# Forgetting attention: copying and scaling both halves of a unit's output at once, the second half added in DRAM by an accumulating transfer

## Chip, cores and metric

The kernel runs on one core of a Trainium2 chip. The metric is the device time of one execution in microseconds (us), as a median over runs. The engines are TensorE (PE, with its weight loads PEld), VectorE (DVE), ScalarE (ACT), GpSimd (POOL) and SyncE (SP), which issues most DMAs.

## What is computed

One layer of an encoder trunk on a sequence of 2048 tokens of width 1024: a mixing block of two halves (eight heads of "forgetting" attention and a multi-scale pool), attention over 256 memory tokens, and a gated feed-forward block. The change concerns the eight heads only:

```python
def forgetting_attention(q, k, v, f_logit):      # q, k, v: (B, H, S, Dh), here H = 8, S = 2048, Dh = 64
    c = cumsum(log_sigmoid(f_logit))
    for start in range(0, S, Q_BLOCK):           # causal: keys up to the query
        s = einsum('bhqd,bhkd->bhqk', qb, kb) * scale
        s = s + c[:, :, start:end, None] - c[:, :, None, :end]
        p = softmax(where(kpos <= qpos, s, -inf))
        outs.append(einsum('bhqk,bhkd->bhqd', p, vb))
```

## The kernel before

All products are computed in float32 accuracy from pairs of words: a number is split into a rounded high part and a low part that holds the rest, and a product is a sum of matmuls of the parts.

The attention stage, some 380 us of the program, works through 32 units, one for each head h (0 to 7) and each block b (0 to 3) of 512 queries. A unit has two sides. On the score side (score_items), for each 128 queries and each 512 keys, PE makes a tile of scores (L791), VectorE adds the forgetting term and tracks the row's extreme (L793, over several chunks reduced by L798), and ACT takes the exponential with row sums (L803). POOL cuts the causal mask into the forgetting term (cm, L782). On the value side (value_items), for each 128 keys, PE turns the weights (tp, L56), ACT casts the high part ph from PSUM (L891), VectorE subtracts the low part pl (L64), and PE multiplies both with the values into an accumulator acc (L854). Of every eighth chunk ACT copies the weights (pf, L887) and POOL makes both parts (L888, and L64 on POOL). The last chunk of a unit covers only 128 of its 256 columns, so POOL zeroes the others of ph and pl beforehand (L880).

A head's values are stored with 128 columns: 64 for the high part of the values and 64 for the low part. So rows 0 to 63 and rows 64 to 127 of acc are two addends of one result, and something has to add them. When a unit's last chunk is multiplied, finish copies rows 64 to 127 to SBUF on ACT (fo, L830) and adds rows 0 to 63 on VectorE (L831). Later scale multiplies fo by 1/l, the inverse of the row sums, on POOL (L837), and POOL's own queue writes it to the DRAM tensor catT (L839), one tensor for each b, 64 rows for each head. After attention the output projection reads catT (load_cat, L736).

The inverse takes a way of its own: POOL adds two partial sums (li, L817), VectorE takes the reciprocal (L818), SP stores the column to DRAM (ld, L819) and reads it back as a row broadcast to all partitions (lbs, L825).

What sets the order: PE, DVE and ACT run in the order in which the code issues (in_order). A loop takes a score item and a value item in turn, the scores 22 items ahead, and each item is a tick. Work can be put off by a number of ticks with later(n, fn): a scale comes 12 ticks after finish, the broadcast load 22 after the reciprocal. POOL and SP aren't in that list: a scheduler places their instructions by priority and readiness when the program is built. Each engine then executes its own list strictly in order, and an instruction that waits for a semaphore holds everything behind it on that engine.

Also on SP: the loads of the next head's queries, keys and forgetting row (L588 to L592, issued with unit (h, 1)) and of the next head's values (L582, unit (h, 3)).

Of the kernel before, what the change touches and what calls it, by code (L numbers as in the profile page):

```python
# [8 lines left out]
F32 = mybir.dt.float32  # L9
F32R = mybir.dt.float32r  # L10
AF = mybir.ActivationFunctionType
ALU = mybir.AluOpType
# [4 lines left out]
P = 128  # L17
# [4 lines left out]
H = 8  # L22
DH = 64
# [18 lines left out]
def block_kernel(ctx: ExitStack, tc: tile.TileContext, x, xT, memT, cols, rows, w_qkvf, w_p, w_pool, w_out,  # L42
# [4 lines left out]
    act, dve, pool, pe, sp = nc.scalar, nc.vector, nc.gpsimd, nc.tensor, nc.sync  # L47

    def opened(stack, name, bufs=1, **kw):
        return stack.enter_context(tc.tile_pool(name=name, bufs=bufs, reuse_waits="tile", **kw))  # L50
# [61 lines left out]
    ld = [dr.tile([P, 4], F32, name=f"ld{n}") for n in range(4 * H)]  # L112
    mkvd = dr.tile([4, P, 1024], F32, name="mkvd")
    catT = [dr.tile([FOXW, 512], F32, name=f"catT{n}") for n in range(4)]
# [605 lines left out]

    EX, X2, INV = 7, 2, 2

    BACK, SCALE = 22, 12

    SHARE = 8

    rest, last_parts = [], []
    hpb = opened(hps, "hpb")
# [14 lines left out]
    with ExitStack() as c0:  # L743
        spool = opened(c0, "spool")
        tpool = opened(c0, "tpool")
# [5 lines left out]
        def later(n, fn):  # L751
            due.append([n, fn])
# [16 lines left out]
        def score_items(unit):  # L769
# [6 lines left out]
            for q in range(4):  # L776
# [8 lines left out]
                for c in range(b + 1):  # L785
# [9 lines left out]
                    if c == b:  # L795
# [11 lines left out]
                        if n > 1024:  # L807
                            later(EX + X2, lambda expo=expo: expo(g=1))
                    yield True
            later(EX + X2 + INV, lambda: inverse(unit))  # L810

        def inverse(unit):

            h, b = unit["u"]
            l = unit["l"]
            li = tpool.tile([P, 4], F32, tag="li", name="li", bufs=8)
            pool.tensor_tensor(out=li[:], in0=l[:, :, 0], in1=l[:, :, 1], op=ALU.add)  # L817
            dve.reciprocal(li[:], li[:])  # L818
            sp.dma_start(ld[4 * h + b], li[:])  # L819
            later(BACK, lambda: inverse_back(unit))  # L820

        def inverse_back(unit):
            h, b = unit["u"]
            unit["lb"] = lbs = tpool.tile([DH, 512], F32, tag="lbs", name="lbs", bufs=3)
            sp.dma_start(lbs[:], ld[4 * h + b].rearrange("t q -> (t q)").partition_broadcast(DH))  # L825

        def finish(unit, acc):
            h, b = unit["u"]
            fo = tpool.tile([DH, 512], F32, tag="fo", name="fo", bufs=3)
            act.copy(fo[:], acc[DH:, :])  # L830
            dve.tensor_tensor(out=fo[:], in0=acc[:DH, :], in1=fo[:], op=ALU.add)  # L831
            later(SCALE, lambda: scale(unit, fo))

        def scale(unit, fo):
            h, b = unit["u"]

            pool.tensor_tensor(out=fo[:].rearrange("p (q t) -> p q t", q=4), in0=fo[:].rearrange("p (q t) -> p q t", q=4),  # L837
                               in1=unit["lb"][:].rearrange("p (t q) -> p q t", q=4), op=ALU.mult)
            pool.dma_start(catT[b][h * DH:(h + 1) * DH, :], fo[:])  # L839

        nchunk = [0]

        def value_items(unit):
# [20 lines left out]
            for j in range(nk):  # L864
# [18 lines left out]
                lag = LAG  # L883
                if nchunk[0] % SHARE == 0 and 0 < j < nk - 4 and not (h == H - 1 and b >= 2):
                    lag += 2
# [11 lines left out]
            def drain():  # L897
                step(True)
                finish(unit, acc)
# [728 lines left out]
```

## Time and profile before

| what | value |
|---|---|
| median of 3 runs | 2525.05 us (2523.53 to 2525.37) |
| the profiled execution | 2526.31 us |
| its span, first to last instruction | 2524.6 us |
| PE, DVE, ACT, POOL busy over the span | 99%, 67%, 49%, 32% |
| granted clock of PE | 1.00 |
| attention, first score matmul to last value matmul | 520.9 to 901.0 us |

The profile is one execution seen by the hardware profiler. Its timeline rows give start, duration, engine, line, operation and what is written from what, then in brackets the engine's idle time before the row and who ended it. Its table of waits has the total, the number of times and the longest. Its table of groups has the number of instructions, busy time and mean in ns, then idle time before them. PE's matmuls are pipelined: a 512-column matmul is shown as 0.39 us or more, though the next may start 0.23 us after it, so PE's pace is read from the distances of starts, not from durations. POOL's spans are rough.

### The profile page before, as it was taken

How to read it: one execution, taken by the hardware profiler on the slowest of the kernel's cores; microseconds unless marked ns; L12 is line 12 of the kernel's file. 1: busy time of each engine (PE TensorE's matmuls, PEld its weight loads, DVE VectorE, ACT ScalarE, POOL GpSimd, SP SyncE). 2: the span in 40 equal slices, each digit the busy share in tenths (PEclk: the TensorE clock that was granted, in tenths of full speed). 3: DMA queues.
4: the chain of work that ended last, by engine and by line, in shares of the span. 5: the costliest groups of instructions: out<-in, count | busy, mean ns of one | idle time of the engine just before them, and what ended most of it. 6: DMA issues, size and time to landing. Idle time of an engine off the chain costs nothing.

```text
span 2524.6 us, 36797 instructions
## 1 busy us (share of the span) xinstructions
PE 2501.6 (99%) x13055; PEld 2139.0 (85%) x13055; DVE 1690.1 (67%) x2999; ACT 1241.4 (49%) x2355; POOL 796.4 (32%) x1096
## 2 busy tenths in 40 slices
PE   9999999999999999999999999999999999999999
PEld 8999999878888878888888888888888888888887
DVE  7444485579999965445877887756776666665554
ACT  6454451069999945444544433335543333333443
POOL 3344310035554623334244554430011212212000
PEclk9999999999999999999999999999999999999999
DMA  6454474364464241223654544457673323325665
GB/s 248 155 156 129 126 240 163 130 180 136 114 170 126 72 134 69 87 88 105 226 203 155 200 163 179 167 190 267 231 254 109 113 96 125 113 96 186 234 205 204
DMA packets 204504, 400.38 MB, mean 159 GB/s; under 512 B 24480, under 2 KB 100000, under 8 KB 193440
## 3 DMA queue, kind: packets, MB, share of 16 engines
q1 hardware_dynamic: 175104, 301.54, 37.0%
q0 software_dynamic: 29216, 96.49, 9.9%
q8 instruction: 102, 1.67, 0.3%
q14 instruction: 82, 0.67, 0.1%
HBM read 273.05 MB, written 129.11 MB: 159 GB/s over the span
## 4 chain that ended last, share of the span: by engine, by line
PE 70%; issue 9%; DVE 3%; ACT 2%; POOL 1%; DMA 0%; SPq 0%; POOLq 0%; DVEq 0%; ACTq 0%
PE bk L71 14%; PE bk L69 14%; PE bk L70 14%; PE acc L854 5%; PE sps L791 4%; PE tp L56 3%; PE mmps L69 3%; PE mmps L71 3%; PE mmps L70 3%; PE oo L69 1%; PE oo L70 1%; PE oo L71 1%; PE zp L69 1%; PE zp L70 1%; PE zp L71 1%
## 5 line engine op out<-in xcount | busy, mean ns | idle before, releaser
L64 DVE TENSOR_TENSOR ww<-draw,ww 128x512 fp32r<-128x512 f32 x308 | 204.6, 702 | 157.2 <-ACT ww L190 156.9
L190 ACT CAST ww<-draw 128x512 fp32r<-128x512 f32 x308 | 179.1, 620 | 220.4 <-PE bk L71 177.7
L64 DVE TENSOR_TENSOR ww<-graw,ww 128x512 fp32r<-128x512 f32 x220 | 177.6, 814 | 107.5 <-ACT ww L190 107.3
L69 PE MATMUL bk<-ww,ww 128*128 128x512 f32 x616 | 239.6, 389 | 0.0
L70 PE MATMUL bk<-ww,ww 128*128 128x512 f32 x616 | 239.6, 389 | 0.0
L71 PE MATMUL bk<-ww,ww 128*128 128x512 f32 x616 | 239.6, 389 | 0.0
L190 ACT CAST ww<-graw 128x512 fp32r<-128x512 f32 x220 | 136.0, 622 | 177.2 <-PE bk L71 159.8
L64 DVE TENSOR_TENSOR pl<-tp,ph 128x512 fp32r<-128x512 f32 (+3 forms) x298 | 177.2, 598 | 16.6 <-ACT ph L891 15.3
L69 PE MATMUL zps<-wh,xhi 128*128 128x384 f32 (+1 forms) x512 | 174.4, 341 | 0.6 <-DVE qs L186 0.6
L70 PE MATMUL zps<-wl,xhi 128*128 128x384 f32 (+1 forms) x512 | 171.9, 336 | 0.0
L71 PE MATMUL zps<-wh,xl 128*128 128x384 f32 (+1 forms) x512 | 171.9, 336 | 0.0
L891 ACT CAST ph<-tp 128x512 fp32r<-128x512 f32 (+3 forms) x298 | 147.9, 517 | 12.2 <-PE tp L56 9.0
L69 PE MATMUL bk<-qs,ww 128*128 128x512 f32 x352 | 137.9, 392 | 0.8 <-ACT s L1440 0.8
L1521 POOL DMA_DIRECT2D out_dram<-o x32 | 17.3, 542 | 382.7 <-DVE o L1518 377.0
L71 PE MATMUL bk<-qs,ww 128*128 128x512 f32 x352 | 137.2, 390 | 0.8 <-DVE ww L64 0.8
L70 PE MATMUL bk<-kh,ww 128*128 128x512 f32 x352 | 137.0, 389 | 0.0
L69 PE MATMUL bk<-kl,ww 128*128 128x512 f32 x352 | 136.9, 389 | 0.0
L70 PE MATMUL bk<-cb,ww 128*128 128x512 f32 x352 | 136.9, 389 | 0.0
L71 PE MATMUL bk<-kl,ww 128*128 128x512 f32 x352 | 136.9, 389 | 0.0
L69 PEld LDWEIGHTS bk<-ww,ww 128*128 128x128 f32 x616 | 115.6, 188 | 24.2
L71 PEld LDWEIGHTS bk<-ww,ww 128*128 128x128 f32 x616 | 115.6, 188 | 24.1
L70 PEld LDWEIGHTS bk<-ww,ww 128*128 128x128 f32 x616 | 115.6, 188 | 23.8
(635 smaller groups left out, 7238.5 us busy)
## 6 DMA issues: line engine op xcount, KB each, us to landing
graw<-in_w_gu_dram SPq DMA_DIRECT2D x44, 1024.0 KB, 5.4
draw<-in_w_down_dram SPq DMA_DIRECT2D x66, 256.0 KB, 4.3
xl<-in_xT_dram SPq DMA_DIRECT2D x64, 256.0 KB, 5.1
qkT<-st SPq DMA_DIRECT2D x64, 256.0 KB, 2.7
wdr<-in_w_down_dram SPq DMA_DIRECT2D x22, 512.0 KB, 4.4
vd<-cb SPq DMA_DIRECT2D x16, 512.0 KB, 3.3
qs<-qkT SPq DMA_DIRECT2D x8, 1024.0 KB, 7.0
kh<-qkT SPq DMA_DIRECT2D x16, 512.0 KB, 9.7
```

Of the source, the lines that this page charges most:

```text
L56: return pe.transpose(out.bitcast(F32R), src, identr[:])
L64: (eng or dve).tensor_tensor(out=lo, in0=src, in1=f(hi), op=ALU.subtract)
L69: pe.matmul(ps, lhsT=sh, rhs=mh, start=first, stop=False, skip_group_check=goes_on)
L70: pe.matmul(ps, lhsT=sh, rhs=ml, start=False, stop=False, skip_group_check=goes_on)
L71: pe.matmul(ps, lhsT=sl, rhs=mh, start=False, stop=last, skip_group_check=goes_on)
L190: act.copy(hi, raw)
L791: pe.matmul(ps[:, :wn], lhsT=qs[:, i * P:(i + 1) * P], rhs=kk[:, 512 * c:512 * c + wn], start=(a == 0), stop=(a == 1))
L854: pe.matmul(acc[:, qa * P:], lhsT=v[:, j, :], rhs=pm[:, qa * P:], start=state["n"] == 1, stop=state["n"] == 2 * nk)
L891: act.copy(ph[:, sl], tp[:, sl])
L1521: pool.dma_start(out[rows_, cs], o)
```

## The change

For the heads 0 to 6 (28 units) ACT copies all 128 rows of acc at once, and VectorE's add is left out. POOL scales all 128 rows, for which the broadcast of 1/l now goes to 128 partitions. SP writes the first 64 rows plainly to catT; 8 ticks after that POOL issues a transfer of the other 64 rows to the same place, which adds to what is there. This transfer must wait until SP's write has landed. Head 7 keeps the old way. The reciprocal and the store of its result come 4 ticks later than before, and the broadcast load 18 ticks after that instead of 22, so at the same tick.

```diff
-    BACK, SCALE = 22, 12
-
-    SHARE = 8
+    BACK, SCALE, ADDED = 22, 12, 8
+
+    SHARE, RECIP = 8, 4
...
-            dve.reciprocal(li[:], li[:])
-            sp.dma_start(ld[4 * h + b], li[:])
-            later(BACK, lambda: inverse_back(unit))
+
+            def turned_over():
+                dve.reciprocal(li[:], li[:])
+                sp.dma_start(ld[4 * h + b], li[:])
+                later(BACK - RECIP, lambda: inverse_back(unit))
+
+            later(RECIP, turned_over)
...
-            unit["lb"] = lbs = tpool.tile([DH, 512], F32, tag="lbs", name="lbs", bufs=3)
-            sp.dma_start(lbs[:], ld[4 * h + b].rearrange("t q -> (t q)").partition_broadcast(DH))
+            unit["lb"] = lbs = tpool.tile([P, 512], F32, tag="lbs", name="lbs", bufs=3)
+            sp.dma_start(lbs[:], ld[4 * h + b].rearrange("t q -> (t q)").partition_broadcast(P))
...
-            fo = tpool.tile([DH, 512], F32, tag="fo", name="fo", bufs=3)
-            act.copy(fo[:], acc[DH:, :])
-            dve.tensor_tensor(out=fo[:], in0=acc[:DH, :], in1=fo[:], op=ALU.add)
+            fo = tpool.tile([P, 512], F32, tag="fo", name="fo", bufs=3)
+            if h < H - 1:
+                act.copy(fo[:], acc[:])
+            else:
+                act.copy(fo[:DH], acc[DH:])
+                dve.tensor_tensor(out=fo[:DH], in0=acc[:DH], in1=fo[:DH], op=ALU.add)
...
-            pool.tensor_tensor(out=fo[:].rearrange("p (q t) -> p q t", q=4), in0=fo[:].rearrange("p (q t) -> p q t", q=4),
-                               in1=unit["lb"][:].rearrange("p (t q) -> p q t", q=4), op=ALU.mult)
-            pool.dma_start(catT[b][h * DH:(h + 1) * DH, :], fo[:])
+            rows = P if h < H - 1 else DH
+
+            pool.tensor_tensor(out=fo[:rows].rearrange("p (q t) -> p q t", q=4), in0=fo[:rows].rearrange("p (q t) -> p q t", q=4),
+                               in1=unit["lb"][:rows].rearrange("p (t q) -> p q t", q=4), op=ALU.mult)
+            cat = catT[b][h * DH:(h + 1) * DH, :]
+            (sp if h < H - 1 else pool).dma_start(cat, fo[:DH])
+            if h < H - 1:
+                later(ADDED, lambda: pool.dma_start(cat, fo[DH:], accum_op=ALU.add))
```

What it moves on the engines, first POOL, where the units (h, 3) and (h + 1, 0) end. catT_118 and catT_115 are the DRAM tensors of block 3 and block 0; li and l belong to the row sums, cm is the mask. Before:

```order
L880 MEMSET ph 128x128
L837 TENSOR_TENSOR fo<-fo,lbs 64x512
L839 DMA catT_118<-fo 64x512
L880 MEMSET pl 128x128
L782 AFFINE_SELECT cm<-cb 128x384
L817 TENSOR_TENSOR li<-l 128x4
L837 TENSOR_TENSOR fo<-fo,lbs 64x512
L773 MEMSET l 128x8
L839 DMA catT_115<-fo 64x512
L888 TENSOR_TENSOR ph<-pf,ones 128x512
L782 AFFINE_SELECT cm<-cb 128x512
L64 TENSOR_TENSOR pl<-pf,ph 128x512
```

And now, where L850 is the accumulating transfer, L845 the scale and L891 the memset (L880 before):

```order
L845 TENSOR_TENSOR fo<-fo,lbs 128x512
L891 MEMSET ph 128x128
L891 MEMSET pl 128x128
L782 AFFINE_SELECT cm<-cb 128x384
L845 TENSOR_TENSOR fo<-fo,lbs 128x512
L850 DMA catT_118<-fo 64x512
L817 TENSOR_TENSOR li<-l 128x4
L773 MEMSET l 128x8
L782 AFFINE_SELECT cm<-cb 128x512
L899 TENSOR_TENSOR ph<-pf,ones 128x512
L64 TENSOR_TENSOR pl<-pf,ph 128x512
L850 DMA catT_115<-fo 64x512
```

The scale stands ahead of both memsets, the DMA issue that stood between them is gone, and the accumulations come behind the next scale and behind the shared chunk; the memsets of unit (h, 1) follow right after the last row shown.

On SP, before (ld_85 to ld_88 hold 1/l of the units (0, 3), (1, 0), (1, 1) and (1, 2), lbs is the broadcast, v the values, catT_117 the tensor of block 2):

```order
L819 DMA ld_85<-li 128x4
L819 DMA ld_86<-li 128x4
L825 DMA lbs<-ld_85 64x512
L825 DMA lbs<-ld_86 64x512
L819 DMA ld_87<-li 128x4
L825 DMA lbs<-ld_87 64x512
L582 DMA v<-vd 128x2048
L819 DMA ld_88<-li 128x4
L825 DMA lbs<-ld_88 64x512
```

And now, with the plain writes of catT (L848) among them:

```order
L821 DMA ld_85<-li 128x4
L821 DMA ld_86<-li 128x4
L848 DMA catT_117<-fo 64x512
L829 DMA lbs<-ld_85 128x512
L829 DMA lbs<-ld_86 128x512
L821 DMA ld_87<-li 128x4
L582 DMA v<-vd 128x2048
L829 DMA lbs<-ld_87 128x512
L848 DMA catT_118<-fo 64x512
L848 DMA catT_115<-fo 64x512
L821 DMA ld_88<-li 128x4
L829 DMA lbs<-ld_88 128x512
```

Each plain write waits for a scale on POOL and stands ahead of broadcasts; the write of block 3 is behind the load of the values.

On VectorE only the add goes and the reciprocals shift by a few rows; the end of unit (0, 0), as a difference:

```order
 L793 ISA s3g_5485,mx<-sps,cb 128x512
 L793 ISA mx 128x1
-L831 TENSOR_TENSOR fo<-acc,fo 64x512
 L64 TENSOR_TENSOR pl<-tp,ph 128x512
 L793 ISA s3g_5485,mx<-sps,cm 128x128
```

The low part (L64) now follows the scores' row directly. ACT's and PE's orders are unchanged.

## The prediction

> **What bounds the kernel now.** First the page: TensorE (PE) is busy all the time, so only time in which PE stands still inside the attention stage can be won or lost.
>
> ```profile
> span 2524.6 us, 36797 instructions
> PE 2501.6 (99%) x13055; PEld 2139.0 (85%) x13055; DVE 1690.1 (67%) x2999; ACT 1241.4 (49%) x2355; POOL 796.4 (32%) x1096
> ```
>
> The span is 2524.6 us of an execution of 2526.3; the median of the runs shown is 2525.05, so I add the sum's difference to that median. 0.2% of it is 5.05 us, about what a measurement of this kernel can tell from no change.
>
> Next the busy times by stretch inside attention (520 to 901 us). Columns: the stretch, its length, then PE, PEld, DVE, ACT and POOL busy.
>
> ```profile
> 660.00:700.00 40.00, 39.83 (x256) 33.31 (x254) 38.30 (x124) 36.32 (x78) 21.26 (x41) 1.00 0.40 127
> ```
>
> Three engines are nearly full: PE 39.8, DVE 38.3 and ACT 36.3 of 40 us; the clock is full (1.00). POOL is half idle. Third, who waited for whom over five heads (586 to 818 us):
>
> ```profile
> PEld tp L56 <- DVE pl L64: 4.3, 15, 0.4
> PEld acc L854 <- POOL pl L880: 1.9, 5, 0.4
> ```
>
> PE's losses are two a head: once on POOL's memset (L880), and on VectorE's low part (L64). The timeline of head 3 gives their size. PE at the last value chunk of the unit (h, 0), and POOL there:
>
> ```profile
> 675.67 1.57 POOL L837 TENSOR_TENSOR fo<-fo,lbs 64x512 f32<-64x512 f32 x1 [1.51 <-DVE fo L831]
> ...
> 677.54 0.57 POOL L839 DMA_DIRECT2D catT<-fo  x1 [0.29 <-POOL fo L837]
> ...
> 677.94 0.28 PE L854 MATMUL acc<-ph,v 128*128 128x256 f32 x1
> ...
> 678.11 0.22 POOL L880 MEMSET pl<- 128x128 f32 x1
> ...
> 678.38 0.39 PE L854 MATMUL acc<-pl,v 128*128 128x256 f32 x1 [0.16 <-POOL pl L880]
> ...
> 678.61 0.46 PE L56 MATMUL tp<-identr,s1g 128*128 128x128 f32 x4
> ```
>
> Matmuls of 256 columns otherwise start 0.12 us apart; this one comes 0.44 after the last and the next 0.23 later: 0.43 us lost, because the scale and the DMA issue stand ahead of the memset. The other loss comes at 704:
>
> ```profile
> 702.31 0.58 ACT L830 COPY fo<-acc 64x512 f32<-64x512 f32 x1
> ...
> 702.92 1.07 ACT L891 CAST ph<-tp 128x512 fp32r<-128x512 f32 x2
> 702.93 0.68 DVE L831 TENSOR_TENSOR fo<-acc,fo 64x512 f32<-64x512 f32 x1
> ...
> 703.54 0.69 DVE L64 TENSOR_TENSOR pl<-tp,ph 128x512 fp32r<-128x512 f32 x1
> ...
> 703.73 0.34 PE L791 MATMUL sps<-kh,qs 128*128 128x384 f32 x1
> ...
> 703.90 0.34 PE L791 MATMUL sps<-kl,qs 128*128 128x384 f32 x1
> ...
> 704.29 0.54 PE L56 MATMUL tp<-identr,s3g 128*128 128x128 f32 x4
> ```
>
> A 384-column matmul needs 0.17 us before its successor (703.73 to 703.90), and the next one gets 0.39: with the late transposes about 0.25 us are lost. The low part at 703.54 ends it, and the final add L831 stands directly ahead of it. But the low part also needs the high part that ACT casts from 702.92, behind its own copy of the output. A cast of 512 columns takes 0.59 (row 679.82 below), so the first of the two in that row ends at 703.51, and the low part starts at 703.54. Without the add it would start 0.03 us earlier. **The add is hidden behind ACT's cast.** What is late here is ACT. Its waits between 674 and 705:
>
> ```profile
> 674.28 0.59 ACT L830 COPY fo<-acc 64x512 f32<-64x512 f32 x1 [0.71 <-PE acc L854]
> ...
> 683.03 1.15 ACT L803 ACTIVATE s3g<-s3g,mx 128x1024 f32<-128x1024 f32 x1 [0.46 <-DVE mx L798]
> ...
> 686.88 1.15 ACT L803 ACTIVATE s3g<-s3g,mx 128x1024 f32<-128x1024 f32 x1 [0.31 <-DVE mx L798]
> ...
> 692.18 1.15 ACT L803 ACTIVATE s3g<-s3g,mx 128x1024 f32<-128x1024 f32 x1 [0.34 <-DVE mx L798]
> ```
>
> These four are all the idle spells that the view marks there. ACT waits for PE at 674.28 and then for nothing but VectorE until PE runs into it at 704.29. One head earlier the same stall stood here:
>
> ```profile
> 657.93 0.54 PE L56 MATMUL tp<-identr,s3g 128*128 128x128 f32 x4
> ```
>
> A head thus takes 704.29 - 657.93 = 46.36 us, and for 30 of them the pace is ACT's, with PE a little ahead; only the 16 from 657.93 to 674.28 are PE's.
>
> **The change part by part.** *VectorE's add* (28 of 32 go):
>
> ```profile
> L837 POOL TENSOR_TENSOR fo<-fo,lbs 64x512 f32<-64x512 f32 x32 | 50.6, 1582 | 39.3 <-DVE fo L831 39.3
> L888 POOL TENSOR_TENSOR ph<-pf,ones 128x512 fp32r<-128x512 f32 x22 | 23.1, 1051 | 0.5 <-ACT pf L887 0.2
> L831 DVE TENSOR_TENSOR fo<-acc,fo 64x512 f32<-64x512 f32 x32 | 21.8, 680 | 1.0 <-ACT fo L830 1.0
> ```
>
> 28 x 0.68 = 19.0 us of VectorE go. Of this little reaches PE. I walked the four adds of a head; the last is shown above, another one here. Behind each stands a low part whose cast runs beside the add (here it ends at 680.41, the low part starts at 680.45), and what it gains the next low part that waits for ACT takes back:
>
> ```profile
> 679.82 0.59 ACT L891 CAST ph<-tp 128x512 fp32r<-128x512 f32 x1
> 679.85 0.68 DVE L831 TENSOR_TENSOR fo<-acc,fo 64x512 f32<-64x512 f32 x1
> ...
> 680.45 0.68 DVE L64 TENSOR_TENSOR pl<-tp,ph 128x512 fp32r<-128x512 f32 x1
> ...
> 681.62 0.69 DVE L64 TENSOR_TENSOR pl<-tp,ph 128x512 fp32r<-128x512 f32 x1 [0.29 <-ACT ph L891]
> ```
>
> At 704 the gain is 0.03: 7 x 0.03 = **0.2 us**. The moved reciprocal is the same instruction a few rows later; its result waits on nothing that PE needs.
>
> *ACT's copy* of 128 rows for 64: ACT casts 512 columns of 128 rows from PSUM in 0.59 us (679.82, above) and copies 64 rows in 0.58 (702.31): 28 x 0.01 = 0.3 us, within ACT's waits, so nothing.
>
> *POOL's scale* of 128 rows is not in the trace. Bounds: 1.05 us (the fastest 128x512 row, L888) and 3.2 (twice L837); I take 1.58, that of the same pattern on 64 rows. It starts when ACT's copy ends (674.87) and not VectorE's add (675.58), and no DMA issue stands between it and the memsets. By the rows the memset of pl then ends near 676.9, where PE asks for it at 678.06: the 0.43 us stall goes. Even at 3.2 us it ends at 678.4, as now. But PE, 0.43 us earlier, meets ACT at 704 in an unmoved place: the stall there grows from 0.25 to about 0.7. **The saving is given back within the head**: 0.
>
> *The accumulating DMA* on POOL isn't in the trace either. Its issue is bounded by the fastest plain issue and by POOL's longest row on the same tile (min/median/max in ns):
>
> ```profile
> L837 POOL TENSOR_TENSOR fo<-fo,lbs x32: 1547/1568/2012, 546.9 to 902.7; 64x512 f32<-64x512 f32 x32
> L839 POOL DMA_DIRECT2D catT<-fo x32: 565/572/707, 548.8 to 905.0; - x32
> ```
>
> So 0.565 to 2.01 us; I take 0.57, the plain median, since it is the nearest in kind. What stands behind it on POOL shows now in these rows:
>
> ```profile
> 681.20 0.20 POOL L817 TENSOR_TENSOR li<-l 128x4 f32<-128x4 f32 x1 [2.41 <-ACT s2g L803]
> ...
> 683.22 0.57 POOL L839 DMA_DIRECT2D catT<-fo  x1 [0.25 <-POOL l L773]
> ...
> 686.76 0.20 POOL L880 MEMSET pl<- 128x128 f32 x1
> ```
>
> From the issue's end (683.79) to the end of the memset pair of unit (h, 1) (686.96) the shared chunk, a mask and the pair take 3.17 us. The second scale, no longer behind li, ends near 681.4 (ACT's copy before the cast of 679.82, plus 1.58). Then 0.57 for the first accumulation, 0.2 each at most for li and l, 3.17, and 0.57 for the second accumulation ahead of the pair: 686.1. PE wants that pair here, or 0.43 earlier, at 687.34:
>
> ```profile
> 687.77 0.28 PE L854 MATMUL acc<-pl,v 128*128 128x256 f32 x1
> ```
>
> So it is hidden, with 1.24 us over. *Its wait* is for SP's plain write to land:
>
> ```profile
> v<-vd SPq DMA_DIRECT2D x5, 1024.0 KB, 4.8
> catT<-fo POOLq DMA_DIRECT2D x20, 128.0 KB, 2.4
> ```
>
> A scale that ends at 676.5 has its write issued by about 677, behind the values' load (issued 674.28, landed near 679.1), so landed near 681; POOL comes to the accumulation at 681.4. Close, but covered. While SP waits for a scale it holds back broadcasts of 1/l (now 256 KB instead of 128) and the next head's loads; for the first nobody waits today (all 39.3 us before L837 are VectorE's add), and the loads are for a head whose scores begin most of 46 us later.
>
> *The last heads.* Here POOL also splits output weights, and PE's loss holds ACT up:
>
> ```profile
> 865.50 0.39 PE L854 MATMUL acc<-pl,v 128*128 128x256 f32 x1 [0.56 <-POOL pl L880]
> 865.92 0.59 ACT L830 COPY fo<-acc 64x512 f32<-64x512 f32 x1 [0.64 <-PE acc L854]
> ```
>
> The scale now comes ahead of a split that waits for ACT, and the DMA issue goes behind the memsets: PE idles 0.56 us there and gets to 865.50 at least so much earlier. ACT was free 0.64 us before its copy at 865.92, and the chain after it is ACT's and VectorE's: **0.6 us** pass on. Sum: 0.2 + 0.6 = 0.8 us; 2525.05 - 0.8 = **2524.2 us**.
>
> **The rivals.** *A, the savings pass in full*: if ACT's chain shifts with PE after all, 7 x 0.43 + 0.8 = 3.8 us: 2521.2. For it: the wait on POOL is plain to see. Against: ACT never waits for PE between 674 and 704. *A2*, VectorE's relief moves ACT too and the 0.25 at 704 goes as well, 7 x 0.25 more: 2519.5. The 0.31 to 0.46 us that ACT waits for VectorE speak for it; the low parts that wait for ACT, against.
>
> *B, POOL is held by the accumulation*, at its issue or its landing. The pair has 1.24 us until 687.34 and 0.68 (0.43 + 0.25) that ACT's pace leaves PE; two accumulations stand ahead of it, so it decides from 0.57 + 1.92/2 = 1.5 us each. At the upper bound, 2.0, the pair is ready 2 x 1.43 = 2.86 us later and costs 0.94 a head: 7 x 0.94 = 6.6, so 2530.8. For it: each of the 28 is a kind of transfer that the trace lacks, with a landing in its wait. Against: the plain issue takes 0.57 with VectorE full, 0.71 at most. The Trainium skill (SBUF — State Buffer, section "A bandwidth-pool intuition that's wrong (but worth ruling out)") has 0.62 us against 3.1 for a GpSimd-issued DMA beside a VectorE copy that locks the shared port; by that, B would give an estimated 3.1 us each, near 2546. The trace disagrees for plain writes: 572 ns in the median beside a VectorE that is busy 38.3 of 40 us.
>
> *That the change doesn't do what it says* is excluded by the order: the adds are gone.
>
> **How the numbers follow.** Forecast 0.58, A 0.11, A2 0.11, B 0.20. Faster by over 0.2% (under 2520.0) is A2: 0.11. Slower by over 0.2% (over 2530.1) is B: 0.20. Within: 0.69. The range takes A in and B's bound: 2520.0 to 2531.0.
>
> **What would show it.** L831 falls to 4 adds; PE's wait for L880 is gone in the steady heads; PE's wait at the end of unit (h, 1) is longer; heads still come every 46.3 us. Wrong if heads come every 45.8 (A), or if PE or POOL waits at L850 or the second memset pair (B).

## The result and the profile after

The changed kernel takes **2518.27 us** (2518.14 to 2519.99, 9 runs) beside 2524.79 (2523.53 to 2528.03, 9 runs) of the kernel before: a ratio of 0.9974, 95% interval 0.9965 to 0.9982. That is 6.5 us less, where 0.8 was forecast. The profiled execution took 2518.27, its span follows. The page of the changed kernel:

```profile
span 2516.6 us, 36820 instructions
PE 2496.4 (99%) x13055; PEld 2139.7 (85%) x13055; DVE 1674.5 (67%) x2971; ACT 1235.0 (49%) x2355; POOL 800.5 (32%) x1096
```

PE's work is the same 13055 matmuls in the same order, so one can follow a single matmul from run to run. VectorE lost 28 instructions, as said. But **ScalarE (ACT) lost 6.4 us of busy time (1241.4 before) with the same 2355 instructions**, and nothing in the forecast had that.

The table follows single matmuls: the stage from 520.9 to 907.58 in the kernel before (the last is the output projection's first row, 6.5 us behind attention's last value matmul), and the distance between the five repeats of the transpose that came late at 704.29 (611.57 to 843.31 in before; columns: us).

| | before | after | difference |
|---|---|---|---|
| attention stage | 386.71 | 380.05 | -6.66 |
| of it: up to 611.57 | 90.70 | 89.04 | -1.66 |
| five heads, 611.57 to 843.31 | 231.74 | 227.30 | -4.44 |
| from 843.31 on | 64.27 | 63.71 | -0.56 |
| one head | 46.35 | 45.46 | -0.89 |
| all other stages | 2130.53 | 2129.19 | -1.34 |

The other stages are not touched; in the profiles below they lie between 2128.4 and 2130.5, so their 1.3 us is scatter of single executions. The stage's 6.7 us is the effect, and heads come every 45.46 us: the forecast said 46.3, and its rival A 45.8.

Where a head's 0.89 us lay shows in the starts of the same matmuls (means of five heads). 0.30 was lost at the last chunk of the unit (h, 0), behind POOL's memset (0.45 us to the start of its last matmul and 0.23 from there to the next before, 0.19 and 0.19 after). 0.27 was lost at the chunk whose parts POOL makes (the two starts up to 687.06 in head 3: 0.39 and 0.34 us before, 0.23 each after), and 0.21 at the late transposes of 704.29. The rest is spread over places of some 0.05 us. The loss of 0.27 stands in the kernel before's table of waits (586 to 818 us), and the prediction does not count it:

```profile
PEld acc L854 <- POOL pl L64: 2.1, 5, 0.4
```

Five heads, before and then after (stretch, length, busy PE, PEld, DVE, ACT, POOL):

```profile
586.00:818.00 232.00, 230.90 (x1486) 193.68 (x1484) 222.53 (x716) 212.79 (x461) 124.68 (x231) 1.00 0.49 137
```

```profile
583.00:811.00 228.00, 228.00 (x1486) 194.84 (x1485) 212.56 (x700) 208.73 (x464) 130.16 (x231) 1.00 0.64 164
```

By the records PE is busy for the whole stretch. The ends of matmuls are modelled and PE's weight load still waits a little, so this says that not much is left, not that nothing is. The waits of the changed kernel in it (who waited for whom: us, times, longest):

```profile
ACT s3g L803 <- DVE mx L798: 5.8, 14, 0.5
...
PEld tp L56 <- DVE pl L64: 1.7, 10, 0.2
POOL catT L850 <- DMA catT<-fo: 1.5, 3, 0.7
```

PE's waits for POOL are gone here, and those for VectorE's low part fell from 4.3 to 1.7. At the end of the unit (h, 1), where PE lost 0.25 us at 704.29, PE of the changed kernel now runs through, with 0.18 us from start to start:

```profile
699.79 0.34 PE L791 MATMUL sps<-kh,qs 128*128 128x384 f32 x1
699.97 0.34 PE L791 MATMUL sps<-kl,qs 128*128 128x384 f32 x1
700.15 0.49 PE L56 MATMUL tp<-identr,s3g 128*128 128x128 f32 x4
```

And ScalarE at the same place. First the kernel before, then the changed one:

```profile
702.08 0.21 ACT L803 ACTIVATION_READ_ACCUMULATOR s0g<-s0g,mx 128x1 f32 x1
702.31 0.58 ACT L830 COPY fo<-acc 64x512 f32<-64x512 f32 x1
702.92 1.07 ACT L891 CAST ph<-tp 128x512 fp32r<-128x512 f32 x2
```

```profile
698.15 0.20 ACT L803 ACTIVATION_READ_ACCUMULATOR s0g<-s0g,mx 128x1 f32 x1
698.25 0.58 ACT L835 COPY fo<-acc 128x512 f32<-128x512 f32 x1
698.71 1.10 ACT L902 CAST ph<-tp 128x512 fp32r<-128x512 f32 x2
```

Read the starts, not the durations, which are equal. Neighbours on ScalarE overlap: an instruction of the changed kernel starts 0.1 us before the one ahead has ended, and the next comes 0.46 after it. The old copy starts 0.02 us *after* the end of the one ahead, and its successor 0.61 after it. Over all copies that did not wait: 0.024 us after the end and 0.608 to the next start before, 0.094 us before the end and 0.467 after. Each old copy thus took **0.26 us more of ScalarE** than the new one, 1.04 us in every head of four units, and its duration shows none of it.

On POOL the changed kernel goes as forecast:

```profile
671.68 1.57 POOL L845 TENSOR_TENSOR fo<-fo,lbs 128x512 f32<-128x512 f32 x1 [1.57 <-ACT fo L835]
673.20 0.20 POOL L891 MEMSET ph<- 128x128 f32 x1
673.34 0.20 POOL L891 MEMSET pl<- 128x128 f32 x1
```

The scale of 128 rows takes 1.57 us, and the memset is done at 673.54, where PE comes to its last chunk at 674.66. The two writes (min/median/max in ns):

```profile
L848 SPq DMA_DIRECT2D catT<-fo x28: 445/459/1307, 547.5 to 855.4; - x28
L850 POOL DMA_DIRECT2D catT<-fo x28: 834/856/925, 551.2 to 858.9; - x28
```

### The profile page after: what moved, and what is told of

It reads as the page before. It is cut to its first block, busy times and chain, and to the rows that moved or that the text cites. A ratio compares the mean times of both kernels' runs of the same rounds, so it can differ in the third digit from the quotient of the medians.

```text
span 2516.6 us, 36820 instructions
## 1 busy us (share of the span) xinstructions
PE 2496.4 (99%) x13055; PEld 2139.7 (85%) x13055; DVE 1674.5 (67%) x2971; ACT 1235.0 (49%) x2355; POOL 800.5 (32%) x1096
## 4 chain that ended last, share of the span: by engine, by line
PE 72%; issue 9%; DVE 2%; POOL 1%; ACT 1%; DMA 1%; POOLq 0%; SPq 0%; ACTq 0%; DVEq 0%
PE bk L71 14%; PE bk L69 14%; PE bk L70 14%; PE acc L865 5%; PE sps L791 5%; PE tp L56 4%; PE mmps L69 3%; PE mmps L71 3%; PE mmps L70 3%; PE oo L69 1%; PE oo L70 1%; PE oo L71 1%; PE zp L69 1%; PE zp L70 1%; PE zp L71 1%
## 5 line engine op out<-in xcount | busy, mean ns | idle before, releaser
L64 DVE TENSOR_TENSOR ww<-draw,ww 128x512 fp32r<-128x512 f32 x308 | 205.2, 705 | 156.1 <-ACT ww L190 155.8
L64 DVE TENSOR_TENSOR ww<-graw,ww 128x512 fp32r<-128x512 f32 x220 | 176.7, 809 | 108.5 <-ACT ww L190 108.2
L64 DVE TENSOR_TENSOR pl<-tp,ph 128x512 fp32r<-128x512 f32 (+3 forms) x298 | 177.5, 599 | 25.8 <-ACT ph L902 25.0
```

The lines of the kernel that those rows point to most:

```text
L64: (eng or dve).tensor_tensor(out=lo, in0=src, in1=f(hi), op=ALU.subtract)
```

## The experiments

**Theory 1**: the old copy, which took the accumulator's rows 64 to 127 down to rows 0 to 63 (a "turned" copy or a "shift" below), stood alone on ScalarE; its 0.26 us a unit set the pace. **Theory 2**: VectorE's relief from the add did it. **Theory 3**: POOL's stall was lifted and passes on in full (rival A). All results first; "before beside it" is the kernel before, timed along with each, "head" the five-head mean as above, "copy" the start after the end of the one ahead and the distance to the next start. Head, stage and copy are each from one profiled execution. Runs 2, 4 to 8 and 12 leave out half of the output (4, 5, 7 and 12 count the other half twice); they are there to separate causes.

| kernel | us | before beside it | ratio, 95% | head | stage | copy |
|---|---|---|---|---|---|---|
| before | | | | 46.35 | 386.71 | +0.024, 0.608 |
| changed | 2518.27 | 2524.79 | 0.9974 [0.9965, 0.9982] | 45.46 | 380.05 | -0.094, 0.467 |
| 1 shift moved to VectorE | 2524.72 | 2524.66 | 1.0000 [0.9991, 1.0009] | 46.34 | 385.99 | -0.096, 0.467 |
| 2 no add | 2524.62 | 2524.66 | 0.9998 [0.9989, 1.0007] | 46.38 | 385.80 | +0.024, 0.609 |
| 3 write by SP | 2531.08 | 2524.66 | 1.0025 [1.0016, 1.0034] | 46.39 | 386.36 | +0.024, 0.609 |
| 4 changed, turned copy | 2525.11 | 2524.66 | 1.0001 [0.9993, 1.0010] | 46.37 | 386.29 | +0.024, 0.608 |
| 5 before, no shift | 2518.81 | 2524.53 | 0.9977 [0.9968, 0.9986] | 45.70 | 381.39 | -0.095, 0.468 |
| 6 no shift, no add | 2516.64 | 2524.53 | 0.9967 [0.9956, 0.9979] | 45.42 | 378.60 | -0.096, 0.467 |
| 7 changed, 64 rows | 2518.01 | 2524.53 | 0.9974 [0.9964, 0.9985] | 45.41 | 379.68 | -0.094, 0.466 |
| 8 no accumulation | 2524.32 | 2524.53 | 0.9999 [0.9990, 1.0008] | 45.42 | 379.64 | -0.094, 0.465 |
| 9 changed, extra copy | 2527.00 | 2525.20 | 1.0007 [0.9997, 1.0016] | 46.73 | 388.27 | -0.094, 0.466 |
| 10 changed, all heads | 2519.20 | 2525.20 | 0.9979 [0.9970, 0.9988] | 45.46 | 380.27 | -0.094, 0.466 |
| 11 half by SP | 2530.05 (1 run) | 2525.20 | | 46.37 | 386.24 | +0.024, 0.609 |
| 12 upper rows, not turned | 2525.40 | 2524.54 | 1.0003 [0.9994, 1.0012] | 46.36 | 386.27 | +0.024, 0.607 |

### 1. The shift moved from ScalarE to VectorE

```diff
-            act.copy(fo[:], acc[DH:, :])
-            dve.tensor_tensor(out=fo[:], in0=acc[:DH, :], in1=fo[:], op=ALU.add)
+            act.copy(fo[:], acc[:DH, :])
+            dve.tensor_tensor(out=fo[:], in0=acc[DH:, :], in1=fo[:], op=ALU.add)
```

> The kernel before, with one edit: ScalarE copies the first 64 rows of the accumulator straight (rows 0-63 to rows 0-63) instead of the second 64 turned down by 64 rows, and VectorE's add takes the second 64 rows from PSUM in their place. Nothing is left out. Theory 1 (the turned copy stood alone on ScalarE: 0.61 us to the next start and 0.02 us after the end of the one before, where the copy of 128 rows in the changed kernel takes 0.47 and begins 0.09 us inside the one before; 0.26 us a unit, 1.0 us a head): the copy's next start comes at 0.47 us, PE's two losses behind ScalarE and VectorE (0.25 and 0.13 us a head) go, the two behind GpSimd (0.28 and 0.22) stay: 7 x 0.38 = 2.7 us, 2522.1 beside a before of 2524.8. Theory 2 (the relief is VectorE's, which lost its add): no change, 2524.8. Theory 3 (GpSimd's two losses pass in full and nothing else matters): no change. If the copy's slot stays 0.61 us, the 64 rows and not the turn are what is slow.

ScalarE's slot fell to 0.47 us, so 64 rows are not slow in themselves. The time did not move: theory 1, as put, failed. The profile of this kernel says why. VectorE:

```profile
701.02 0.15 DVE L798 TENSOR_REDUCE mx<-mx 128x1 f32<-128x2 f32 x1
701.20 0.69 DVE L831 TENSOR_TENSOR fo<-acc,fo 64x512 f32<-64x512 f32 x1
701.93 0.69 DVE L64 TENSOR_TENSOR pl<-tp,ph 128x512 fp32r<-128x512 f32 x1
```

The add, now the one that reads from row 64, stands alone in its turn: it starts 0.03 us after the end of the one ahead, and the low part comes 0.73 us after it. In the kernel before, those were 0.08 us before the end and 0.60: VectorE pays 0.23 us a unit. PE's late transpose stands where it stood, now 0.4 us late, and waits for that low part, which begins as soon as VectorE is free. One engine was relieved by 0.26 us and the other burdened by 0.23; the experiment moved the cost and did not take it away.

### 2. The add alone

```diff
-            dve.tensor_tensor(out=fo[:], in0=acc[:DH, :], in1=fo[:], op=ALU.add)
```

> The kernel before without VectorE's final add; the first half of every output is left out. ScalarE's copy stays turned. Theory 1: GpSimd's scale starts 0.6 us earlier, so the losses behind GpSimd (0.28 and 0.22 us a head) go, but ScalarE sets the pace and PE loses the same again at the end of the unit (h, 1): 0 to 1 us gained, 2523.8 to 2524.8. Theory 2: VectorE's relief speeds the rowwise minima for which ScalarE waits, all four losses go, 7 x 0.88 = 6.2 us: 2518.6. Theory 3: GpSimd's losses go and pass on, 7 x 0.5 = 3.5 us: 2521.3.

No gain, and heads at 46.38: theories 2 and 3 fall. VectorE had 0.6 us a unit to spare and waited with it for ScalarE. In the five heads of this kernel (the kernel before had 8.7 us in 32 waits):

```profile
DVE pl L64 <- ACT ph L890: 19.7, 55, 0.6
PEld tp L56 <- DVE pl L64: 6.0, 20, 0.4
```

This is what the prediction said of the add: hidden behind ScalarE's cast.

### 3. POOL's stall alone

```diff
-            pool.dma_start(catT[b][h * DH:(h + 1) * DH, :], fo[:])
+            (sp if h < H - 1 else pool).dma_start(catT[b][h * DH:(h + 1) * DH, :], fo[:])
```

> The kernel before with the plain write of the scaled output issued by SP instead of GpSimd (heads 0 to 6); nothing is left out, ScalarE and VectorE do what they did. GpSimd loses 0.87 us a unit between the scale and the memsets. This is the step of the prediction by itself (a GpSimd stall removed is given back at the end of the unit (h, 1)). Theory 1 and the prediction: the losses behind GpSimd go (0.50 us a head) and the one at the end of the unit (h, 1) grows from 0.25 to about 0.7: 2524.0 to 2524.8. Theory 3: 7 x 0.5 = 3.5 us pass on, 2521.3, and heads come every 45.86 us. Theory 2: like theory 1, since VectorE keeps its add.

Heads at 46.39 and a stage shorter by only 0.35 us: with the slow copy, what POOL gives back is lost again, and theory 3 falls a second time. But the places are not quite the one forecast. The end of the unit (h, 0), POOL, then VectorE, then PE's weight load:

```profile
676.56 0.21 POOL L880 MEMSET pl<- 128x128 f32 x1
```

```profile
677.20 0.28 DVE L64 TENSOR_TENSOR pl<-tp,ph 128x128 fp32r<-128x128 f32 x1
```

```profile
677.60 0.19 PEld L854 LDWEIGHTS acc<-pl,v 128*128 128x128 f32 x1 [0.21 <-issue]
```

The memset is done at 676.77, 0.4 us before PE asks. Yet PE's load of that chunk still comes 0.40 us after the one ahead, since the rest of the same tile, VectorE's low part behind ScalarE's casts, ends at 677.48 only. In the kernel before, it ended at 678.11 and the memset at 678.33: the profile names whoever comes last, and 0.2 us behind POOL stood ScalarE's chain. So of the 0.30 us at this chunk 0.16 is won and 0.14 stays. The 0.27 at POOL's own chunk goes too. By the starts of the same matmuls both come back in the rest of the head: 0.20 us at the last chunk of the unit (h, 1), 3 us ahead of 704.29, and 0.12 at two transposes in between. The stall at 704.29 itself stayed near 0.2 us.

The run as a whole is slower by 6.4 us, outside attention and behind PE's last matmul: see the last section.

### 4. The changed kernel with the old copy

```diff
-                act.copy(fo[:], acc[:])
+                act.copy(fo[:DH], acc[DH:])
...
-            rows = P if h < H - 1 else DH
+            rows = DH
...
-                later(ADDED, lambda: pool.dma_start(cat, fo[DH:], accum_op=ALU.add))
+                later(ADDED, lambda: pool.dma_start(cat, fo[:DH], accum_op=ALU.add))
```

> The changed kernel with ScalarE's copy turned again: the second 64 rows of the accumulator go to rows 0-63, GpSimd scales 64 rows, and both transfers write these rows, so the first half of the output is left out and the second counted twice. VectorE has no add, GpSimd's order is that of the changed kernel. Theory 1: the slot is 0.61 us again, ScalarE falls back to its old pace and PE loses most of the 0.88 us a head again at the ends of the units (h, 1): 2522 to 2524.5. Theories 2 and 3: the time of the changed kernel, 2518.3.

2525.11 us, heads at 46.37: with VectorE's add gone, POOL in its new order and both transfers in place, this one copy gives the whole gain back. Theory 1 stands for ScalarE, but run 1 needs an addition: VectorE can hold the heads at the same pace. Hence theory 4 (no shift on either engine is enough) against theory 5 (VectorE's add has to go too).

### 5. No shift on either engine

```diff
-            act.copy(fo[:], acc[DH:, :])
+            act.copy(fo[:], acc[:DH, :])
```

> The kernel before with no operand turned anywhere: ScalarE copies the first 64 rows straight, and VectorE adds the same first 64 rows from PSUM; the first half of the output is counted twice and the second left out. All instructions of the kernel before are there. In the run with the add turned instead of the copy, ScalarE's slot fell from 0.61 to 0.47 us and VectorE's add went from 0.60 to 0.72 and began after the one before it had ended. Theory 4 (the turn takes some 0.25 us a unit from whichever of the two engines does it, and either of them alone can hold the heads at 46.36 us): with the turn gone from both, ScalarE is relieved by 1.0 us a head and VectorE is as before; gain between 2.7 us (0.38 a head) and 6.2 (0.88): 2518.5 to 2522. Theory 5 (both engines have to be relieved, VectorE of the add as well): 2524.7, heads at 46.36 still.

2518.81 us, the stage shorter by 5.32 us where the change has 6.66, with the add, the old order of POOL and no second transfer. Theory 4 holds: **four fifths of the gain come with the copy's 0.26 us alone**. What is left is 0.24 us a head (45.70 against 45.46). By the starts of the matmuls it lies at the last chunk of (h, 0), whose low part comes 0.27 us later than in the changed kernel, and PE's wait for POOL's memset stands in this run as it stood before:

```profile
PEld acc L854 <- POOL pl L880: 1.9, 5, 0.4
```

The changed kernel has neither the DMA issue ahead of this memset nor the add ahead of the scale; now that ScalarE is fast, the stall counts.

### 6. No shift and no add

```diff
-            act.copy(fo[:], acc[DH:, :])
-            dve.tensor_tensor(out=fo[:], in0=acc[:DH, :], in1=fo[:], op=ALU.add)
+            act.copy(fo[:], acc[:DH, :])
```

> The kernel before with ScalarE's copy of the first 64 rows straight and without VectorE's add; the second half of every output is left out. GpSimd scales 64 rows and issues its plain write as before. Theories 4 and 5: ScalarE and VectorE are relieved as in the changed kernel, so PE's losses behind them go, and those behind GpSimd shrink since the scale starts 0.6 us earlier: 2518 to 2520, heads near 45.5. If GpSimd's issue ahead of the memsets matters by itself, PE still loses 0.3 us a head there: 2520.5. If neither matters without the move of the write: 2524.7.

2516.64 us, less than expected, and heads at 45.42, close to those of the changed kernel: the scale starts before the add would have ended, and POOL's DMA issue, still ahead of the memsets, no longer holds PE. So without the add the stall goes even with the issue there:

```profile
672.38 1.57 POOL L836 TENSOR_TENSOR fo<-fo,lbs 64x512 f32<-64x512 f32 x1 [1.61 <-ACT fo L830]
674.25 0.57 POOL L838 DMA_DIRECT2D catT<-fo  x1 [0.30 <-POOL fo L836]
674.96 0.22 POOL L879 MEMSET pl<- 128x128 f32 x1
```

The stage is 1.45 us below the changed kernel's; 1.3 of that lie from 843.31 on (62.42 us for 63.71), where the changed kernel has the old path in the last head. It leaves out half of the output, so it is a bound and not a better kernel.

### 7. The changed kernel on 64 rows

```diff
-                act.copy(fo[:], acc[:])
+                act.copy(fo[:DH], acc[:DH])
```

with the edits of run 4 on `rows` and the accumulation.

> The changed kernel with 64 rows for 128 and no turn: ScalarE copies the first 64 rows straight, GpSimd scales them, and both transfers write these rows (the first half counted twice, the second left out). It differs from the run with the turned copy, which took 2525.1, by the turn alone. Theory of the turn: the time of the changed kernel, 2518.3, copy slots of 0.47 us, heads at 45.5. If the number of rows is what counts, and not the turn: 2525.

2518.01 us. Against run 4 only the rows that ScalarE reads differ (0 to 63 for 64 to 127), PE, VectorE, ScalarE and POOL have the same lists in the same order, and 7.1 us lie between them. ScalarE of run 7:

```profile
697.38 0.20 ACT L803 ACTIVATION_READ_ACCUMULATOR s0g<-s0g,mx 128x1 f32 x1
697.47 0.57 ACT L835 COPY fo<-acc 64x512 f32<-64x512 f32 x1
697.94 1.07 ACT L902 CAST ph<-tp 128x512 fp32r<-128x512 f32 x2
```

### 8. No accumulating transfer

```diff
-            if h < H - 1:
-                later(ADDED, lambda: pool.dma_start(cat, fo[DH:], accum_op=ALU.add))
```

> The changed kernel without the accumulating transfer; the second half of the output is left out (heads 0 to 6). The accumulation's price as GpSimd and the queues pay it: if hidden, as predicted, heads stay at 45.5 and the attention stage ends within 0.3 us of the changed kernel. One thing may cover it: where SP wrote the plain kernel's output, and GpSimd issued 28 transfers less, GpSimd's drain at the very end took 9.0 us for 3.1 and the run 6.4 us more; if this hangs on the number of GpSimd's transfers, this run has it too: 2524 to 2525. Else 2518.3.

Heads at 45.42 and a stage of 379.64 for 380.05: 28 accumulations cost 0.4 us at most, hidden as forecast. The run's 6 us more are the drain of run 3 again.

### 9. ScalarE's time put back in another way

```diff
                 act.copy(fo[:], acc[:])
+                more = tpool.tile([P, 256], F32, tag="more", name="more", bufs=1)
+                act.copy(more[:], acc[:, :256])
```

> The changed kernel with one instruction more on ScalarE behind each of the 28 straight copies: 256 columns of the accumulator, straight, into a tile that nobody reads. By the casts of 256 columns (next start 0.25 us later) it takes what the turn took. If it is ScalarE's time alone by which the turn cost, heads come every 46.3 to 46.4 us again and the run takes 2524 to 2525.5. If the turn does something else (holds the PSUM bank or VectorE up), the time stays that of the changed kernel, 2518.3, with heads at 45.46.

The extra copy has its successor 0.262 us later, just what the old copy took beyond the new one, and overlaps like any other. It reads rows 0 to 127, so no shift is left in it:

```profile
702.69 0.58 ACT L835 COPY fo<-acc 128x512 f32<-128x512 f32 x1
703.15 0.39 ACT L837 COPY more<-acc 128x256 f32<-128x256 f32 x1
703.42 1.10 ACT L904 CAST ph<-tp 128x512 fp32r<-128x512 f32 x2
```

Three of the five heads take 46.46 to 46.53 us, about four times 0.26 more than the 45.46 of the changed kernel. The other two take 46.92 and 47.27: there PE also lost 0.7 and 1.1 us to POOL's share of the chunks, and the time, 2527.0 us, is 1.5 above the range expected. The rows of POOL show why:

```profile
644.61 1.04 POOL L901 TENSOR_TENSOR ph<-pf,ones 128x512 fp32r<-128x512 f32 x1 [0.30 <-ACT pf L900]
647.54 0.86 POOL L852 DMA_DIRECT2D catT<-fo  x1 [1.89 <-PE tp L56]
648.13 1.58 POOL L64 TENSOR_TENSOR pl<-pf,ph 128x512 fp32r<-128x512 f32 x1
```

In this kernel an accumulation stands between the high and the low part of the shared chunk, once a head, where the changed kernel has it behind both (POOL is placed anew when a program is built). The plain write of the same rows, issued by SP at 643.55, took 3.5 us to land, at 647.02. POOL's wait for that landing ends at 647.04, and the accumulation follows 0.5 us behind it, as elsewhere; the row names PE only because one of its semaphores came last. It is the wait of rival B, and it reaches PE in two heads of five. So this run changes more than ScalarE's time; its three other heads, and that the profile shows no wait of PE for a copy of acc, say that it is ScalarE's time by which the old copy cost, whatever takes it.

### 10. The new path for the last head too

```diff
-            if h < H - 1:
+            if h < H:
```

and so in the three other places.

> The changed kernel with the new path for the last head too: no turned copy and no add is left, and GpSimd still issues 354 transfers. By ScalarE's time (4 x 0.26 us) and the run without any turn or add, in which the stage from the last head on took 62.4 us for 63.7, up to 1.3 us: 2517.0. If the last accumulations, 8 ticks late and some 3 to 4 us to landing, are waited for by the output projection's first load: 2518.3 to 2521.

2519.20 us; from 843.31 on 63.94 us for 63.71. The better case did not come. At the end of the stage (880 to 930 us) the accumulations wait for the plain writes to land, and PE behind the projection's first rows:

```profile
POOL catT L850 <- DMA catT<-fo: 5.6, 2, 2.8
...
PEld mmps L69 <- DVE h L1148: 2.2, 1, 2.2
```

That this wait of PE, 1.6 us longer than in the changed kernel by the starts of its matmuls, comes from the accumulations was not tried. Of the kernels here that write the whole output the changed kernel as it is has the lowest median, though this run's interval overlaps with its own.

### 11. Half of the writes by SP

```diff
-            pool.dma_start(catT[b][h * DH:(h + 1) * DH, :], fo[:])
+            (sp if h % 2 == 0 else pool).dma_start(catT[b][h * DH:(h + 1) * DH, :], fo[:])
```

> The kernel before with the plain writes of heads 0, 2, 4 and 6 issued by SP, so that GpSimd issues 338 transfers (354 before, 326 in the two runs with a drain of 9.0 us at the end for 3.1). Nothing is left out. If the last drain grows with each transfer that is missing: near 6.5 us. If it has two values: 3.1 or 9.0. Heads at 46.35 in any case, since ScalarE's copy stays turned.

Its drain takes 9.5 us in the one execution there is: more than with fewer transfers, so by these counts it does not grow with the number that is missing. Neither expected value came.

### 12. The upper rows, not turned

```diff
-                act.copy(fo[:DH], acc[:DH])
+                act.copy(fo[DH:], acc[DH:])
...
-            rows = DH
+            rows = slice(DH, P) if h < H - 1 else slice(0, DH)
```

against run 7, and both writes from these rows.

> The run on the first 64 rows (changed kernel, straight copy, 2518.0) with the second 64 rows in their place: ScalarE copies rows 64-127 to rows 64-127, nothing is turned, GpSimd scales and both transfers write these rows (the second half counted twice, the first left out). What is told apart is why the copy stood alone. If it is the turn (rows in and rows out differ): slots of 0.47 us, heads at 45.4, 2518. If it is the first row, 64 where the instructions before and behind it read and write from row 0: the copy starts 0.024 us after the end of the one before, its next start comes at 0.61 us, heads at 46.36, 2524.5 to 2525.5. Of VectorE the Trainium skill states the second (VectorE: DVE Perf Modes, section Two Vector instructions with no wait between them): an instruction whose operand starts in another group of 32 rows than the last one's in that memory waits for all before it. No page says it of ScalarE.

```profile
701.00 0.20 ACT L803 ACTIVATION_READ_ACCUMULATOR s0g<-s0g,mx 128x1 f32 x1
701.22 0.58 ACT L835 COPY fo<-acc 64x512 f32<-64x512 f32 x1
701.83 1.08 ACT L902 CAST ph<-tp 128x512 fp32r<-128x512 f32 x2
```

The copy stands alone again, 2525.40 us, though nothing is turned: rows 64 to 127 go to rows 64 to 127. So the name "turned copy" was wrong. **What makes it stand alone is that it starts at row 64, among neighbours that start at row 0**; and the neighbour behind, back at row 0, waits in the same way. Whether two instructions that both start at row 64 would overlap, no run shows. A wait of 0.12 us ahead of it and one of 0.14 behind it make the 0.26.

The Trainium skill has a rule of this kind for VectorE, as a model (VectorE: DVE Perf Modes, section "Two Vector instructions with no wait between them"): an instruction is held until all earlier ones have finished if an input starts in another group of 32 rows than the first input of the last instruction that read the same memory, or its output in another than the last output written there. VectorE of run 1 agrees on both sides of the add (0.03 us behind the end ahead, and 0.03 us between its own end and the low part). Here ScalarE behaves alike, with 0.024 us on both sides.

## Why the prediction was wrong

It forecast 2524.2 us, and the time is 2518.3; even the range's low end, 2520.0, is above it. Step by step:

- ACT's copy of 128 rows for 64: *"ACT casts 512 columns of 128 rows from PSUM in 0.59 us (679.82, above) and copies 64 rows in 0.58 (702.31): 28 x 0.01 = 0.3 us, within ACT's waits, so nothing."* **This step failed.** It compared durations. Its own quoted rows had the cost: the copy of 702.31 and the cast of 702.92 lie 0.61 us apart, where the two casts of the same width in the row of 702.92 take 1.07 us together at 0.59 each, so start 0.48 apart. The term is not +0.3 but -28 x 0.26 = -7.3 us, on the very engine that the prediction had named as the pace. Run 5, with that term alone, gains 5.3 us in the stage; runs 4 and 12, without it, 0.4.
- *"What is late here is ACT"; from 674 to 704 "the pace is ACT's".* Right, and it is why most of the missed term reaches the time. Run 9 gives ScalarE its 0.26 us back and has the heads at 46.5 or more.
- *The add is hidden behind ScalarE's cast.* Right: run 2, heads at 46.38 without it.
- *"PE's losses are two a head"*, 0.43 us behind the memset and 0.25 at 704. The first was 0.30 by what the changed kernel has at the same place, and a third, 0.27 at the chunk that POOL makes, was left out.
- *POOL's stall goes and is given back within the head.* The sum is right for the slow copy (run 3), the place only in part: about half of the 0.30 is never won, because the rest of the same chunk was late as well, and what is won comes back between 681 and 701.5, not at 704.29. In the changed kernel, with a faster ScalarE, it does pass on: run 5, which still has the stall, is 0.24 us a head behind.
- *The scale takes 1.58 us, the accumulation is hidden.* Right: 1.57 us; run 8. The issue takes 0.86 us and not 0.57, still below the 1.5 at which rival B would have decided. B's 2530.8 did not come, nor the 3.1 us a transfer that the prediction took from the Trainium skill (SBUF — State Buffer, section "A bandwidth-pool intuition that's wrong (but worth ruling out)"); that section speaks of a VectorE copy, and VectorE runs none in these heads, so its case does not occur here. POOL did wait at L850, in 6 of 28 cases, which the prediction had called a sign of B; PE did not feel it in the five heads of the changed kernel, but did in two heads of run 9.
- *0.6 us at the last heads.* Right in size: 0.56 us from 843.31 on, and 0.52 in run 4, so it is not the copy's.
- Rival A2 (2519.5) came nearest in time and had the wrong cause: VectorE's relief moves nothing by itself (run 2); only with the fast copy is it worth 0.28 us a head (run 6 beside run 5). That ScalarE itself would be relieved was not among the cases.

Why three different loads (the old copy, run 1's add, the old copy without an add) all hold the heads at 46.34 to 46.39 us is not settled. That ScalarE and VectorE hand each chunk to and fro (cast, low part, minimum, exponential) so that 0.25 us on either lengthens one chain fits runs 1, 2 and 5; it was not shown by itself.

## What to carry to other kernels

Where an engine sets the pace, cost its instructions by the distance from start to start and not by their durations: here an instruction that started at row 64 among neighbours at row 0 lost the overlap on both sides, and a small instruction that is "the same length" was worth a quarter of a microsecond each time. Moving such an operand to VectorE moved the cost along with it; copying all 128 rows from row 0, and giving the shift to a transfer, removed it. A stall that is given back under one pace-maker can pass on in full once that pace-maker is faster, so terms that hide behind an engine have to be summed again after every change to it.

## What the runs showed that was not expected

Behind PE's last matmul, POOL drains its queue before the kernel ends (a DRAIN instruction in its list). With 354 transfers issued by POOL this took 3.03 to 3.13 us in all eleven kernels. With 326 (runs 3 and 8) it took 8.97 us in both, with 338 (run 11) 9.46, and the runs were longer by some 6 us for it, though the last output transfer was issued at 2518.43 in run 3 and at 2520.70 in the kernel before. The change replaces 28 of POOL's writes by 28 of POOL's accumulations and so keeps 354. What the drain waits for, and which counts are short, stays open.

The accumulating transfer's issue took 0.86 us in the median beside 0.57 for a plain one on the same queue, and it landed 4.4 us after it in the median (2.5 for the plain ones before, 3.1 for SP's plain write in the changed kernel). POOL waited for the plain write's landing in 6 of 28 cases, 4.9 us in all.
